# Loops exchanged so that products with 64 output rows alternate between the two halves of the array

## The chip, the cores and the metric

The kernel runs on one core of one Trainium2 chip. The number that counts is the device time of one execution in microseconds (us). Five engines work side by side and meet at semaphores: TensorE (PE, matrix products into PSUM, with its weight loads listed apart as PEld), VectorE (DVE), ScalarE (ACT), GpSimd (POOL) and SyncE (SP, which issues most transfers). TensorE is granted a clock at one of two levels, 2.4 GHz (shown as 1.00) or 1.2 GHz (0.50).

## What is computed

A two-layer encoder over 512 tokens of width 1024, in float32 at the interface. Layer 0 mixes by a convolution and a state-space model (SSM), layer 1 by attention in a neighbourhood; both end in a gated feed-forward network. Cut to the parts that matter here:

```python
# layer 0: depthwise convolution of width 31, and a scan in two directions
a = za * sigmoid(zg)
a = conv_general_dilated(a, conv_w, feature_group_count=512) + conv_b   # then layer norm, silu
s = associative_scan(affine, (A, B @ u))                                # 32 groups, 64 states
y = einsum(s_re, c_re) - einsum(s_im, c_im)                             # forward + backward, + d * u
# layer 1: 16 heads of 64, a query sees 8 grid rows x 16 grid columns
s = einsum('bhqd,bhjkd->bhqjk', q_r, k_blk) * scale + bias              # masked outside the window
p = softmax(s)
out = einsum('bhqjk,bhjkd->bhqd', p, v_blk)
# both layers
x = x + h;  x = x + (silu(h2 @ w_gate) * (h2 @ w_up)) @ w_down
```

## The kernel before

The program is one function, `tile_hybrid_encoder`, with helpers inside it. Its schedule is written by hand: instructions go to each engine's queue in the order of the Python code, and every engine works its queue in that order. A `Background` object only interleaves some VectorE work (the tables `Q` of the SSM output) with the loops, by a running credit. Large products are made in float32 pairs of a rounded part and a rest, three products each (`mm3`); the small products that the change touches are plain float32. In the trace each plain float32 product shows as two records of PE and two of PEld.

Three places make products with 64 output rows. In each, one PSUM tile of 128 partitions holds two independent results: output rows 0 to 63 come from the left half of the array's columns, rows 64 to 127 from the right half.

- **Convolution** (lines 991 to 1009). For each of 16 pairs of channel groups `n`, and for each half `h`, five products over the shifts `l` add up in `ps[64 * h:64 * h + 64, ...]`. The tables `t` (tiles `tca`, `tcb`) are made by ACT (line 763) or, for `TCV = 10`, by DVE (line 775), some groups ahead. After four groups DVE adds the bias (line 1006, tile `an` in the trace) and sums for the layer norm (line 1008).
- **SSM output**, `out_y` (lines 1014 to 1032). For each of four groups `gi` and each half, three products add up: one with the matrix `T` (line 1026) and two with `Q` (line 1028). It is called four times, with the layer norm's steps `ln_mean` and `ln_scale` between the calls; ACT copies the result (line 1031, `yn`).
- **Attention values**, `values` (lines 1372 to 1385). A unit `u` is a head pair `hp` (8 of them) and a quarter `j` of the queries (4), 32 units in all. For each head `e` of the pair, which is one half of the array, two blocks `b` of keys add up. The table `BLK` gives the blocks: for `j` = 1 and 2 both blocks have 128 keys, that is 128 rows of the array; for `j` = 0 the first block and for `j` = 3 the second has 64 keys, 64 rows of the array.

Attention is a pipeline over steps `s` (lines 1470 to 1484). In each step TensorE gets the transposes of unit `s-4` (`transp`, tile `t`, line 1364), the scores of unit `s` (tile `s`, line 1334) and the values of unit `s-6` (tile `o`, line 1379). DVE adds the bias and takes the row extreme (line 1341), ACT makes the exponentials (line 1344), DVE the reciprocal (line 1352) and POOL the scaling (line 1354). The transposed weights are copied to `pt_` (tile `sq`, two buffers) by ACT for `j` = 1, 2 (line 1366) and by DVE for `j` = 0, 3 (line 1369). The copy of unit `u` reuses the buffer of unit `u-2`, so it waits for that unit's values. After a head pair's fourth unit, DVE moves `o` to `qh` and `ql` (lines 1384, 1385). In the last six steps parts of the output projection (tile `wo`, lines 200 to 202) fill in between.

Of the kernel before, what the change touches and what calls it, by code (L numbers as in the profile page):

```python
# [30 lines left out]
P = 128  # L31
# [84 lines left out]
def tile_hybrid_encoder(ctx, tc, x, mix_norm, ffn_norm, ffn_w_gate, ffn_w_up, ffn_w_down,  # L116
# [5 lines left out]
    V, A, PE, PL = nc.vector, nc.scalar, nc.tensor, nc.gpsimd  # L122
# [51 lines left out]
    def psa(name="psa"):  # L174
        return psp.tile([P, 512], F32, tag="a", name=name, bufs=4)

    def psb(name="psb"):
        return psp.tile([P, 512], F32, tag="b", name=name, bufs=4)
# [3 lines left out]
    def xtile(name, dt=F32):  # L182

        i = xslot[0] % 10
        xslot[0] += 1
        if i < 8:
            return xp.tile([P, 512], dt, tag=f"x{i}", name=name)
        if i == 8:
            xpair_[:] = [xp.tile([P, 2, 512], dt, tag="x8", name=name)]
        return xpair_[0][:, i - 8]  # L190
# [83 lines left out]
    class Background:  # L274
# [20 lines left out]
        def tick(self, ns):  # L295
            self.credit = min(self.credit, CAP) + ns * self.share
            while self.credit > 0 and (self.jobs or self.fill):
                if self.jobs:
                    self.step()
                else:  # L300
                    self.step_fill()
# [31 lines left out]
    def pt(shape, name, pool=None, dt=F32):  # L333
        return (pool or mp).tile(shape, dt, tag=name, name=name)
# [274 lines left out]
    ps = psb("vec0")  # L609
# [12 lines left out]
    for k in range(KD):  # L622
        t = xtile("xT")
# [36 lines left out]
    for i in range(4):  # L660
# [7 lines left out]
        for kk in range(2):  # L668
            k = 2 * i + kk
            for j in range(4):  # L670
                c = slice(j * P, (j + 1) * P)
# [5 lines left out]
        if i == 1:  # L677
            make_pb(1)
            make_pb(2)
            ps = psb("vec")  # L680
# [10 lines left out]
            for t in range(LCH):  # L691
                p0 = 64 * (t % 2) + 16 * (t // 2)
# [4 lines left out]
        if i == 2:  # L697
            for r in range(2):
                ps = psb("ct")
# [66 lines left out]
    def make_tc(n):  # L766
        if n != TCV:
            for _ in g_tc(n):
                pass
            return  # L770
        t = slots[n // 2 % 3]
        for i in range(2):
            tcs[n + i] = t[:, :, i]
            for h in range(2):
                V.tensor_tensor(out=t[:, h, i], in0=wvs[:, h, n + i].unsqueeze(1).to_broadcast([P, 16, NLAG]),
                                in1=mask16.unsqueeze(2).to_broadcast([P, 16, NLAG]), op=ALU.mult)
# [10 lines left out]
    U = pt([P, G, NCH], "U")  # L787
# [17 lines left out]
    S2 = pt([P, 2, G, NCH], "S2")  # L805
# [126 lines left out]
    f, b = slice(0, 64), slice(64, 128)  # L932
# [18 lines left out]
    T = xp.tile([P, LCH, G, 16], F32, tag="xgl", name="T")  # L951
# [10 lines left out]
    Q = {i: lp.tile([P, 2, 8, 8, 16], F32, tag="Q", name="Q", bufs=4) for i in (0, 2, 1, 3)}  # L962
# [28 lines left out]
    for b in range(4):  # L991
        ps = psa("conv")
        for gi in range(4):
            n = 4 * b + gi
            t = tcs.pop(n)
            for h in range(2):
                for l in range(5):
                    PE.matmul(out=ps[64 * h:64 * h + 64, gi * P:gi * P + P],
                              lhsT=AC[:, 16 * h + n, l:l + NCH],
                              rhs=t[:, h, :, 8 * l:8 * l + 8],  # L1000
                              start=(l == 0), stop=(l == 4))
            if n % 2 and n + 5 < 16:
                make_tc(n + 5)
            tick(2200)
        gs = slice(4 * b, 4 * b + 4)
        V.tensor_tensor(out=yc[:, :, gs], in0=ps.rearrange("p (g c t) -> p t g c", g=4, t=LCH),
                        in1=cbB[:, gs].unsqueeze(1).to_broadcast([P, LCH, 4, 16]), op=ALU.add)
        V.tensor_reduce(out=lns[:, b], in_=yc[:, :, gs].rearrange("p t g c -> p t (g c)"), axis=AX.X, op=ALU.add)
        bgV.charge(1200)
# [4 lines left out]
    def out_y(i, hq, between=None):  # L1014
        for key in ((i, hq), (i + 2, hq)):
            if key in job_q:
                bgV.finish(job_q[key])
        ps = psb("y")
        for gi in range(4):
            if gi == 2 and between is not None:  # L1020
                between()
            for h in range(2):
                g = h * 16 + i * 8 + hq * 4 + gi
                o = ps[64 * h:64 * h + 64, gi * P:(gi + 1) * P]
                q8 = Q[g // 8]
                PE.matmul(out=o, lhsT=U[:, g], rhs=T[:, :, g], start=True, stop=False)
                for r in range(2):
                    PE.matmul(out=o, lhsT=S2[:, r, g],
                              rhs=q8[:, r, g % 8].rearrange("p t c -> p (t c)"),
                              start=False, stop=(r == 1))  # L1030
        A.activation(out=yn[:, :, i * 8 + hq * 4:i * 8 + hq * 4 + 4],
                     in_=ps.rearrange("p (g t c) -> p t g c", g=4, t=LCH), func=AF.Copy)
# [66 lines left out]
    def out_a(ct):  # L1099
# [9 lines left out]
        V.tensor_tensor(out=mal[:, ct], in0=y, in1=mah[:, ct].bitcast(F32), op=ALU.subtract)  # L1109

    out_y(0, 0)
    ln_mean()
    out_y(0, 1)
    for j in job_q.values():
        bgV.finish(j)
    W.ahead()
    out_y(1, 0, ln_scale)
    out_y(1, 1)
    ygs = mp.tile([P, 2, 4, S], F32R, tag="S2", name="ygs")
# [27 lines left out]
    for p2 in range(2):  # L1147
        wh, wl = W.next()
        W.ahead()
        for mi in range(2):  # L1150
            m = 2 * p2 + mi
            ps = psb("glu")
            for k in (0, 2, 1, 3):
                c = slice(mi * P, mi * P + P)
# [60 lines left out]
    for m in range(KD):  # L1215
        ps = psa("dn")
# [5 lines left out]
        t = xtile("x2")  # L1222
# [40 lines left out]
    def ring(name, dt=F32):  # L1263
        return ap_.tile([P, S], dt, tag="ring", name=name, bufs=6)
# [24 lines left out]
    def qk_post(qs, ssh, cg, psx):  # L1289

        isq = cg < 2
        for hp in range(4):
# [16 lines left out]
    BLK = {0: ((0, 64, 0, 0), (64, 128, 1, 0)), 1: ((0, 128, 1, 0), (128, 128, 2, 0)),  # L1309
           2: ((0, 128, 2, 0), (128, 128, 3, 0)), 3: ((0, 128, 3, 0), (128, 64, 0, 64))}  # L1310
# [61 lines left out]
    def values(u):  # L1372
        hp, j = units[u]
        pt_ = pts.pop(u)
        o = obank[hp % 2]
        for e in range(2):
            for b, (c0, n, kt, p0) in enumerate(BLK[j]):
                hc = (2 * hp + e) * 64
                PE.matmul(out=o[64 * e:64 * e + 64, j * P:(j + 1) * P], lhsT=vt[p0:p0 + n, kt, hc:hc + 64],  # L1379
                          rhs=pt_[p0:p0 + n, b, e], start=(b == 0), stop=(b == 1))  # L1380
        if j == 3:
            ov = o.rearrange("p (a r l) -> p a l r", l=16, r=8)[:, :, ::-1]
            hv, lv = (m_[:, hp].rearrange("p (a l r) -> p a l r", l=16, r=8) for m_ in (qh, ql))
            V.tensor_copy(out=hv, in_=ov)
            V.tensor_tensor(out=lv, in0=ov, in1=hv.bitcast(F32), op=ALU.subtract)

    for n, cg in enumerate(QKV_ORDER):
# [5 lines left out]
        for i in range(4):  # L1393
# [13 lines left out]
            for kk in range(2):  # L1407
                k = 2 * i + kk
                for j in range(4):
# [4 lines left out]
                    else:  # L1414
                        a, b = VSP[j - 1]
# [18 lines left out]
        else:  # L1434
            ssh = tmp([P, 4, 8], "ssh")
            qs = []
            for j in range(4):
                t = ring("qs")
# [31 lines left out]
    for s in range(2, NU + LV):  # L1470
        if 0 <= s - LT < NU:
            transp(s - LT)
        if s < NU:
            scores(s)
        if 0 <= s - LN < NU:
            normalize(s - LN)
        if 0 <= s - LV < NU:
            values(s - LV)
        if s == NU:
            out_proj(0, 0, 2)  # L1480
        if s == NU + 1:
            out_proj(0, 2, 4)
        if s == NU + 2:
            out_proj(0, 4, 7)
# [12 lines left out]
    for h in range(2):  # L1497
        for j in range(4):
            ps = psb("xn3")
# [3 lines left out]
            t = fp.tile([P, 512], F32, tag="xn3", name="xn3", bufs=4)  # L1503
# [3 lines left out]
        for i in range(NF // 2):  # L1507
# [5 lines left out]
            for kk, j in steps:  # L1513
                k = 2 * i + kk
                c = slice(j * P, (j + 1) * P)
# [4 lines left out]
        for j in range(4):  # L1520
            t = xn3[h, j]
# [30 lines left out]
```

## Time and profile before

| | us |
|---|---|
| median of 3 runs | 1246.53 (1246.44 to 1246.9) |
| the profiled execution | 1244.67 |
| its span, first to last instruction | 1242.9 |
| PE busy / PEld busy | 1212.7 / 961.6 |
| DVE busy / ACT busy / POOL busy | 671.6 / 473.8 / 38.5 |
| share of PE in the chain that ended last | 94% |

The span is 1.8 us shorter than the profiled execution's own time. PE busy counts records that overlap once, and their ends are modelled, so a busy PE need not be a PE at its best. The convolution and the SSM output lie between 135 and 193 us of the span, attention's pipeline between 753 and 832 us; the rest is almost all large products.

### The profile page before, as it was taken

How to read it: one execution, taken by the hardware profiler on the slowest of the kernel's cores; microseconds unless marked ns; L12 is line 12 of the kernel's file. 1: busy time of each engine (PE TensorE's matmuls, PEld its weight loads, DVE VectorE, ACT ScalarE, POOL GpSimd, SP SyncE). 2: the span in 40 equal slices, each digit the busy share in tenths (PEclk: the TensorE clock that was granted, in tenths of full speed). 3: DMA queues.
4: the chain of work that ended last, by engine and by line, in shares of the span. 5: the costliest groups of instructions: out<-in, count | busy, mean ns of one | idle time of the engine just before them, and what ended most of it. 6: DMA issues, size and time to landing. Idle time of an engine off the chain costs nothing.

```text
span 1242.9 us, 16156 instructions
## 1 busy us (share of the span) xinstructions
PE 1212.7 (98%) x6427; PEld 961.6 (77%) x6427; DVE 671.6 (54%) x1160; ACT 473.8 (38%) x835; POOL 38.5 (3%) x90
## 2 busy tenths in 40 slices
PE   7999869999999999999999999999999999999998
PEld 4655668888888888888888887678888888888886
DVE  8999787654444444333336654746544444452322
ACT  4556747532333232222234545634332332322120
POOL 1001000000000000000000002420000000000000
PEclk9999989999999999999999999999999999999999
DMA  7411402233333333333345442203233333323331
GB/s 159 92 52 57 118 1 80 91 102 102 94 93 95 92 102 98 93 94 94 102 136 169 136 131 91 86 18 102 85 102 102 102 90 97 90 96 102 119 102 34
DMA packets 173154, 118.04 MB, mean 95 GB/s; under 512 B 21193, under 2 KB 153593, under 8 KB 173080
## 3 DMA queue, kind: packets, MB, share of 16 engines
q1 hardware_dynamic: 172616, 115.92, 32.1%
q10 hardware_dynamic: 400, 1.07, 0.4%
q8 instruction: 50, 0.82, 0.3%
q14 instruction: 24, 0.20, 0.0%
q0 software_dynamic: 64, 0.03, 0.0%
HBM read 109.04 MB, written 7.96 MB: 94 GB/s over the span
## 4 chain that ended last, share of the span: by engine, by line
PE 94%; DVE 3%; ACT 2%; DMA 1%; issue 0%; SPq 0%; POOL 0%; POOLq 0%; DVEq 0%; ACTq 0%
PE up L200 6%; PE gate L201 6%; PE up L201 6%; PE gate L202 6%; PE up L202 6%; PE gate L200 6%; PE qkv L1417 4%; PE qkv L1418 4%; PE qkv L1419 4%; PE dn L202 3%; PE dn L201 3%; PE dn L200 3%; PE dn L1518 3%; PE dn L1516 3%; PE dn L1517 3%; PE o L1379 3%
## 5 line engine op out<-in xcount | busy, mean ns | idle before, releaser
L92 DVE TENSOR_TENSOR wlo<-wraw,whi 128x1024 fp32r<-128x1024 f32 x176 | 213.0, 1213 | 261.2 <-ACT whi L90 259.8
L90 ACT ACTIVATE whi<-wraw 128x1024 fp32r<-128x1024 f32 x176 | 183.4, 1044 | 283.1 <-issue 113.9
L200 PE MATMUL gate<-xgh,whi 128*128 128x512 f32 x352 | 137.2, 390 | 0.0
L200 PE MATMUL up<-xgh,whi 128*128 128x512 f32 x352 | 137.1, 390 | 0.0
L202 PE MATMUL gate<-xgh,wlo 128*128 128x512 f32 x352 | 137.0, 389 | 0.0
L202 PE MATMUL up<-xgh,wlo 128*128 128x512 f32 x352 | 137.0, 389 | 0.0
L201 PE MATMUL gate<-xgl,whi 128*128 128x512 f32 x352 | 136.9, 389 | 0.0
L201 PE MATMUL up<-xgl,whi 128*128 128x512 f32 x352 | 136.9, 389 | 0.0
L1201 DVE TENSOR_TENSOR fu<-up,rstdB 128x512 f32<-128x512 f32 x44 | 30.4, 691 | 113.3 <-PE up L202 113.3
L1203 ACT ACTIVATE gh<-fu 128x512 fp32r<-128x512 f32 x44 | 27.8, 632 | 150.8 <-DVE fu L1202 150.8
L200 PEld LDWEIGHTS gate<-xgh,whi 128*128 128x128 f32 x352 | 66.1, 188 | 13.9
L202 PEld LDWEIGHTS up<-xgh,wlo 128*128 128x128 f32 x352 | 66.1, 188 | 13.7
L201 PEld LDWEIGHTS gate<-xgl,whi 128*128 128x128 f32 x352 | 66.1, 188 | 13.7
L200 PEld LDWEIGHTS up<-xgh,whi 128*128 128x128 f32 x352 | 66.0, 188 | 13.7
L201 PEld LDWEIGHTS up<-xgl,whi 128*128 128x128 f32 x352 | 66.0, 188 | 13.7
L202 PEld LDWEIGHTS gate<-xgh,wlo 128*128 128x128 f32 x352 | 66.0, 188 | 13.6
L200 PE MATMUL dn<-gh,whi 128*128 128x512 f32 x176 | 69.3, 394 | 0.0
L201 PE MATMUL dn<-gl,whi 128*128 128x512 f32 x176 | 69.3, 394 | 0.0
L202 PE MATMUL dn<-gh,wlo 128*128 128x512 f32 x176 | 69.3, 394 | 0.0
L1518 PE MATMUL dn<-whi,gl 128*128 128x512 f32 x176 | 69.2, 393 | 0.0
L1516 PE MATMUL dn<-whi,gh 128*128 128x512 f32 x176 | 69.0, 392 | 0.0
L1417 PE MATMUL qkv<-whi,xgh 128*128 128x512 f32 x176 | 68.8, 391 | 0.0
(296 smaller groups left out, 2057.8 us busy)
## 6 DMA issues: line engine op xcount, KB each, us to landing
wraw<-in_ffn_w_gate_dram SPq DMA_DIRECT2D x44, 512.0 KB
wraw<-in_ffn_w_up_dram SPq DMA_DIRECT2D x44, 512.0 KB
wraw<-in_ffn_w_down_dram SPq DMA_DIRECT2D x38, 512.0 KB
wraw<-in_na_w_qkv_dram SPq DMA_DIRECT2D x24, 512.0 KB
wraw<-in_ab_w_in_dram SPq DMA_DIRECT2D x12, 512.0 KB
bt<-bd SPq DMA_DIRECT2D x8, 640.0 KB
wraw<-in_ab_w_out_dram SPq DMA_DIRECT2D x8, 512.0 KB
wraw<-in_na_w_out_dram SPq DMA_DIRECT2D x8, 512.0 KB
```

What stands on the lines that cost most here:

```text
L90: self.nc.scalar.activation(out=hi, in_=raw, func=AF.Copy)
L92: eng.tensor_tensor(out=lo, in0=raw, in1=hi.bitcast(F32), op=ALU.subtract)
L200: PE.matmul(out=o, lhsT=lh, rhs=rh, start=start, stop=False)
L201: PE.matmul(out=o, lhsT=lh, rhs=rl, start=False, stop=False)
L202: PE.matmul(out=o, lhsT=ll, rhs=rh, start=False, stop=stop)
L1379: PE.matmul(out=o[64 * e:64 * e + 64, j * P:(j + 1) * P], lhsT=vt[p0:p0 + n, kt, hc:hc + 64], rhs=pt_[p0:p0 + n, b, e], start=(b == 0), st ...
L1417: PE.matmul(out=pq[j], lhsT=lh, rhs=wh[:, kk], start=(k == 0), stop=False)
L1418: PE.matmul(out=pq[j], lhsT=lh, rhs=wl[:, kk], start=False, stop=False)
L1419: PE.matmul(out=pq[j], lhsT=ll, rhs=wh[:, kk], start=False, stop=(k == 7))
L1516: PE.matmul(out=pd[j], lhsT=gh[:, k, c], rhs=wh[:, kk], start=(k == 0), stop=False)
L1517: PE.matmul(out=pd[j], lhsT=gh[:, k, c], rhs=wl[:, kk], start=False, stop=False)
L1518: PE.matmul(out=pd[j], lhsT=gl[:, k, c], rhs=wh[:, kk], start=False, stop=(k == NF - 1))
```

## The change

In all three places the loop over the halves becomes the inner one. The same products are made with the same operands, and each half's sum is built in the same order; only the order in which the two halves' products stand in TensorE's queue is new. The queues of DVE, ACT, POOL and SP are the same, instruction by instruction.

```diff
-            for h in range(2):
-                for l in range(5):
+            for l in range(5):
+                for h in range(2):
                     PE.matmul(out=ps[64 * h:64 * h + 64, gi * P:gi * P + P],
...
-            for h in range(2):
-                g = h * 16 + i * 8 + hq * 4 + gi
-                o = ps[64 * h:64 * h + 64, gi * P:(gi + 1) * P]
-                q8 = Q[g // 8]
-                PE.matmul(out=o, lhsT=U[:, g], rhs=T[:, :, g], start=True, stop=False)
-                for r in range(2):
-                    PE.matmul(out=o, lhsT=S2[:, r, g],
-                              rhs=q8[:, r, g % 8].rearrange("p t c -> p (t c)"),
+            gs = [h * 16 + i * 8 + hq * 4 + gi for h in range(2)]
+            o = [ps[64 * h:64 * h + 64, gi * P:(gi + 1) * P] for h in range(2)]
+            for h, g in enumerate(gs):
+                PE.matmul(out=o[h], lhsT=U[:, g], rhs=T[:, :, g], start=True, stop=False)
+            for r in range(2):
+                for h, g in enumerate(gs):
+                    PE.matmul(out=o[h], lhsT=S2[:, r, g],
+                              rhs=Q[g // 8][:, r, g % 8].rearrange("p t c -> p (t c)"),
                               start=False, stop=(r == 1))
...
-        for e in range(2):
-            for b, (c0, n, kt, p0) in enumerate(BLK[j]):
+        for b, (c0, n, kt, p0) in enumerate(BLK[j]):
+            for e in range(2):
                 hc = (2 * hp + e) * 64
                 PE.matmul(out=o[64 * e:64 * e + 64, j * P:(j + 1) * P], lhsT=vt[p0:p0 + n, kt, hc:hc + 64],
```

TensorE's queue at the end of attention, before and then in the change (`t` transposes, `o` values, `wo` output projection; the two last units' values are units 30 and 31). This is the one unit whose waits let the order be seen, since the products of all other units read alike:

```order
@@ -2914,6 +2879,8 @@
 L1379 MATMUL o<-sq,vt 64x128 [waits Activation_49]
 L1379 MATMUL o<-sq,vt 64x128 x3
-L1379 MATMUL o<-sq,vt 64x128 [waits DVE_49] x2
-L1379 MATMUL o<-sq,vt 64x128 x2
+L1379 MATMUL o<-sq,vt 64x128 [waits DVE_49]
+L1379 MATMUL o<-sq,vt 64x128
+L1379 MATMUL o<-sq,vt 64x128 [waits DVE_49]
+L1379 MATMUL o<-sq,vt 64x128
 L200 MATMUL wo<-qh,whi 128x512
 L201 MATMUL wo<-ql,whi 128x512
```

The wait for the second block's copy moved from the second product of unit 31 to the third: both halves of the first block now stand ahead of both halves of the second. The same exchange is made in each of the 32 units.

TensorE's queue at the first call of `out_y`, before (the two buffers of `Q` are those of the two halves):

```order
L1026 MATMUL y_1716<-T_1376,U_523 64x128
L1028 MATMUL y_1716<-Q_1384,S2_524 64x128 x2
L1026 MATMUL y_1716<-T_1376,U_523 64x128
L1028 MATMUL y_1716<-Q_1385,S2_524 64x128 x2
L1026 MATMUL y_1716<-T_1376,U_523 64x128
```

and in the change, where line 1025 is the product with `T`:

```order
L1025 MATMUL y_1716<-T_1376,U_523 64x128 x2
L1028 MATMUL y_1716<-Q_1384,S2_524 64x128
L1028 MATMUL y_1716<-Q_1385,S2_524 64x128
L1028 MATMUL y_1716<-Q_1384,S2_524 64x128
L1028 MATMUL y_1716<-Q_1385,S2_524 64x128
```

Three products of one half and three of the other became six that alternate.

## Rows read from the trace of the kernel before

**Rows 1.** The page: busy time of each engine; shares of the chain by engine.

```profile
PE 1212.7 (98%) x6427; PEld 961.6 (77%) x6427; DVE 671.6 (54%) x1160; ACT 473.8 (38%) x835; POOL 38.5 (3%) x90
...
PE 94%; DVE 3%; ACT 2%; DMA 1%; issue 0%; SPq 0%; POOL 0%; POOLq 0%; DVEq 0%; ACTq 0%
```

**Rows 2.** Windows, one head pair: PE, PEld, DVE, ACT, POOL busy (count), PEclk, DMA share.

```profile
777.20:785.70 8.50, 8.50 (x78) 5.65 (x73) 5.92 (x27) 5.12 (x18) 3.54 (x8) 1.00 0.25 77
```

**Rows 3.** Chain of waits, same head pair: start us, us, what.

```profile
776.85 0.59 PE o L1379 x8
...
778.58 1.44 PE o L1379 x8
...
781.16 1.44 PE o L1379 x8
...
783.70 0.59 PE o L1379 x8
```

**Rows 4.** Timeline of PEld: start, us, line, operation, tiles, array rows*columns.

```profile
781.09 0.19 PEld L1379 LDWEIGHTS o<-sq,vt 64*64 64x64 f32 x2
781.45 0.19 PEld L1379 LDWEIGHTS o<-sq,vt 128*64 128x64 f32 x2 [0.17 <-issue]
...
782.53 0.42 PEld L1364 LDWEIGHTS t<-ident,e 128*128 128x128 f32 x4 [0.17 <-issue]
...
783.63 0.42 PEld L1379 LDWEIGHTS o<-sq,vt 128*64 128x64 f32 x8
```

**Rows 5.** Timeline of PE from 783.62 to 783.70 us, columns as in rows 4.

```profile
783.63 0.34 PE L1379 MATMUL o<-sq,vt 128*64 128x128 f32 x2
```

**Rows 6.** Line 1379: its products by shape; one of those who waited (us, times).

```profile
L1379 PE MATMUL o<-sq,vt x256: 269/273/324, 764.1 to 831.7; 128*64 128x128 f32 x96, 64*64 64x128 f32 x32
...
  DVE sq L1369: 20.1, 8
```

**Rows 7.** Chain of waits at the end of attention.

```profile
830.34 0.43 PE o L1379 x2
...
830.80 1.15 PE o L1379 x6
831.95 0.43 PE wo L200
```

**Rows 8.** Line 998, the convolution: idle of PE before it; who waited (nobody).

```profile
  ACT tca L763: 7.5, 7
  ACT tcb L763: 7.0, 2
who waited for it (us, times):
```

**Rows 9.** Chain of waits around the SSM output.

```profile
181.10 0.59 PE mean L1067 x2
...
187.53 0.60 ACT yn L1031
188.13 0.95 ACT whi L90
...
195.36 1.79 PE cT L1093 x29
```

**Rows 10.** Timeline of PE at the start of the second `out_y`.

```profile
181.63 0.69 PE L1026 MATMUL y<-T,U 128*64 128x128 f32 x2
...
182.11 0.48 PE L1026 MATMUL y<-T,U 128*64 128x128 f32 x1
```

**Rows 11.** Windows around the SSM output, columns as in rows 2.

```profile
180.00:185.00 5.00, 3.90 (x32) 3.87 (x34) 3.37 (x4) 2.01 (x10) 0.00 (x0) 0.50 0.01 3
...
190.00:195.00 5.00, 3.59 (x64) 3.35 (x60) 4.59 (x19) 1.22 (x4) 0.00 (x0) 1.00 0.61 193
195.00:200.00 5.00, 4.64 (x71) 4.33 (x71) 3.22 (x7) 4.92 (x10) 0.00 (x0) 1.00 0.07 22
```

**Rows 12.** Timeline of PE: products with 64 output rows that already alternate between halves.

```profile
122.42 1.15 PE L882 MATMUL v<-U,un_ppb 128*64 128x64 f32 x32
```

## The prediction

> **What bounds the kernel now.** I read the page first. PE is busy for 98% of the span and holds 94% of the chain that ended last [rows 1], so a gain has to be TensorE time at a place where TensorE is what everyone waits for. Busy time alone doesn't tell whether products run side by side, so I went to the three places that the change touches, and at each asked two questions: do the two halves of the array overlap already, and does anyone wait for the result?
>
> Attention. In the windows view TensorE is busy for all 8.50 us that a head pair (four units) takes; DVE has 5.92 us of work in that time, ACT 5.12, POOL 3.54 [rows 2]. The windows of the head pairs before and after it read alike. DVE's copies waited 20.1 us for the values [rows 6]. So TensorE sets the pace. The chain shows what it does with the time: the eight records of one unit's values (four float32 products, two records each) take either 0.59 us or 1.44 us, in the rhythm 0.59, 1.44, 1.44, 0.59 [rows 3]. The weight loads tell the two kinds apart. In a long unit there are four groups of two loads, 0.36 us from one to the next, and the shape changes from 64 to 128 array rows at every group: 781.09, 781.45, and so on to the transposes at 782.53 [rows 4]. These are `j` = 0 and 3, where one block has 64 keys. In a short unit (`j` = 1, 2) all eight loads have 128 rows and go through in one run of 0.42 us [rows 4]. There the two halves do run side by side, although the old order gives all of one half before the other: the first two records, one of each half, together span 0.34 us from their start, hardly longer than the 0.32 that one record lasts at most [rows 5, 6]. So TensorE overlaps halves across several products already. It pays at each change of the number of rows, where nothing of the next shape starts until the last is through.
>
> Convolution. TensorE sat idle for 7.5 and 7.0 us ahead of it until ACT had its tables, and nobody waited for its result [rows 8].
>
> SSM output. After the layer norm's mean product at 181.10 the chain goes through the second call of `out_y`, at the lower clock of 1.2 GHz (granted 0.50 [rows 11]), to ACT's copy `yn` at 187.53, and on through the weight split to the transposes at 195.36 [rows 9]. Here it is on the path.
>
> **The change part by part.** No instruction is added or removed, and only TensorE's queue has another order, so no other queue is passed.
>
> Values, `j` = 1 and 2 (16 units). Eight records already overlap in 0.59 us; both orders have one shape and no change of rows. I take 0 and bound it at 0.1 us a unit either way, 1.6 us in all.
>
> Values, `j` = 0 and 3 (16 units; 32 of the 128 products have 64 rows, two in each of them [rows 6]). The old order has the shapes 64, 128, 64, 128, and at 0.36 us a group that is 4 x 0.36 = 1.44 us. The new order has two groups, each with both halves. If the second half rides along, as in the short units, a group costs its 0.36 plus the lag between halves, 0.02 at most (0.34 less 0.32 [rows 5, 6]); I take 0.37, so the unit costs 0.74 and saves 0.70 us. Bounds: the new unit can't be shorter than a short one, 0.59, which saves 0.85; and each group holds half of a short unit's records, so if it cost as much as a whole short unit, the unit would take 1.18 and save 0.26. I stay with 0.70, since a group of 0.36 is measured with the very shapes, and the overlap with one of them. Over 16 units: 11.2 us, between 4.2 and 13.6.
>
> The Trainium skill, in "TensorE: Matmul & The Clock Gate", part 3 ("What overlaps and what doesn't"), says that a weight load overlaps a running product only where the row groups differ. By that rule two halves that share their rows could not overlap, the new unit would still need its 1.44 us, and the sum would lose the 11.2. The run of eight loads in 0.42 us [rows 4] is against it; the rule is a rival below.
>
> Is the time then TensorE's to give? A head pair shrinks from 8.50 to 8.50 - 2 x 0.70 = 7.10 us. DVE's 5.92 us still fit, with 1.2 to spare, ACT and POOL more easily. DVE waits for the values before its copies for `j` = 0, 3, and the bias steps stand behind these copies in its queue; but TensorE overwrites a unit's scores only two steps later, 2 x 7.10 / 4 = 3.6 us, and the seven records of two copies, two bias steps and a reciprocal are about 1.5 us by DVE's mean of 5.92 / 27 = 0.22 a record [rows 2]. The bias loads use 0.25 of the transfer engines over 8.50 us [rows 2], 2.1 us of 7.10. So I let no other engine take back anything; if DVE's waits bring a head pair to 7.6, eight of them return 4 us. The last unit stands behind DVE's copies: its eight records ran from 830.34 to 831.95, and the second block's copy released the rest at 830.80 [rows 7]. In the new order the first block is through by 830.71 and the second ends at 830.80 + 0.37 = 831.17, again 0.7 earlier.
>
> SSM output. The old order lets the first half run alone until the second half's first product starts 0.48 us later (182.11 against 181.63 [rows 10]). The new one starts both at once, and the call's 48 records end that much sooner: 0.5 us on the chain, bounds 0 and 0.5. The other calls end ahead of ACT's turn. The layer norm's mean, which starts this stretch, waits for DVE and not for TensorE.
>
> Convolution. Alternating shortens its PE time, and all of that falls into PE's idle time [rows 8]: 0. Its cover is ACT's table making; without that cover the convolution would give a few us more, but ACT's order is the same.
>
> Clock. More idle time ahead of the SSM output can change when the clock falls or rises. If the rest of the SSM output and what follows it up to 200 us ran at the lower level, their PE time of 3.59 + 4.64 us [rows 11] could double, of which 5.00 - 3.59 = 1.4 us fall into a wait; at most 6.8 us are lost. If the second `out_y` got the full clock instead, about half of its 5.9 us (181.63 to 187.53 [rows 9, 10]), 2.9 us, would be won. I take 0.
>
> Sum: 11.2 + 0.5 = 11.7 us. Of the profiled execution's 1244.67 us this leaves 1232.97. The median of the runs is 1.86 us above that execution, and the forecast is for the median: 1246.53 - 11.7 = 1234.8 us.
>
> **The rivals.**
> 1. The halves don't overlap at 64 rows. All rows on overlap in line 1379 are for 128 array rows; the 64-row groups never had the other half beside them. Then a 64-row group costs two single ones, 0.72, the unit 1.09, and 16 units save 5.6 us: 1246.53 - 6.1 = 1240.4. For it: that shape is untested. Against it: nothing in the 128-row rows points to a reason.
> 2. Another engine takes over. DVE would go from 70% to 83% of the time; with 4 us returned: 1238.8.
> 3. The lower clock reaches past 188.5 us. At half of the 6.8 us above this gives 1234.8 + 3.4 = 1238.2, at most 1241.6. For it: the SSM stage already has the lower level once, and PE will idle more ahead of it. Against it: before, the clock was back at 1.00 by 190 us [rows 11], while PE worked.
> 4. Nothing happens in attention: halves with equal rows overlap only when a run of one half ends, and the pairs stay one after the other. 1246.53 - 0.5 = 1246.0. The rule of the Trainium skill named above gives this too. Against it: 32 records that alternate went through in 1.15 us [rows 12].
> 5. Slower: each change of half makes TensorE drain, as each change of rows does. The place is `j` = 1 and 2, where the new order has three changes of half instead of one. At 0.36 us a group the unit goes from 0.59 to 1.44, 16 x 0.85 = 13.6 us, and the long units gain nothing: 1246.53 + 13.6 = 1260.1. It decides as soon as a change of half costs over 0.70 / 4 = 0.18 us, since there are two more of them in a short unit and two in a long one, against 0.70 us gained. [rows 12] speak strongly against it, with a product every 0.07 us in alternation.
>
> **How the numbers follow.** Forecast 0.76, rival 1 0.07, rival 2 0.06, rival 3 0.05, rival 4 0.03, rival 5 0.03. The forecast's own bounds are 1246.53 - 13.6 - 0.5 = 1232.4 and, with 0.6 us a unit and nothing from the SSM output, 1236.9; I widen the lower one to 1232 for the clock. The upper end goes to 1240, which takes in rivals 2 and 3 and stops at rival 1. A measurement of this kernel can tell about 0.2% (2.5 us) from no change. Forecast and rivals 1 to 3 are all faster by more than that, 0.94; rival 4 is within it, 0.03; rival 5 slower, 0.03.
>
> **What would show it.** In the changed profile the values of all units should take about 0.59 or 0.74 us in the chain and no longer 1.44, with two groups of four weight loads where there were four of two in the long units; a head pair should take about 7.1 us with PE still busy throughout; the convolution should be shorter and PE's idle time before it longer by as much; the second `out_y` should take about 5.4 us from its first product to `yn`, where it took 5.9. A head pair of over 7.4 us with gaps on PE would speak for rival 2, units of 1.09 for rival 1, a granted clock of 0.50 past 188.5 us for rival 3. The prediction is wrong if two halves with 64 array rows exclude each other, or if alternation itself costs.

## The result, and the profile after

The changed kernel takes 1233.01 us (median of four, 1232.66 to 1234.7) where the kernel before takes 1246.49 (median of four, three of them the runs of the table ahead of the prediction): ratio 0.9897, 95% interval 0.9885 to 0.9909. A second set gives 1233.59 against 1245.84, ratio 0.9902 (0.9887 to 0.9917). It is faster by 13.5 us in the first set and by 12.3 us in the second. The profiled execution took 1232.86 us, its span is 1231.1 us against 1242.9: 11.8 us shorter, where the sum had 11.7. One run of experiment e4 below took 1512.51 us at a mean granted clock of 0.75, and e4's ratio leaves it out.

First the page of the changed kernel: busy time of each engine, and the chain's shares. Compare [rows 1].

```profile
PE 1194.9 (97%) x6427; PEld 949.4 (77%) x6427; DVE 670.8 (54%) x1160; ACT 473.1 (38%) x835; POOL 37.5 (3%) x90
...
PE 94%; DVE 3%; ACT 2%; DMA 0%; issue 0%; SPq 0%; POOL 0%; POOLq 0%; DVEq 0%
```

PE's busy time fell by 17.8 us with the same 6427 records, which is more than the span lost: most of the other 6 us came out where PE waits anyway (the convolution, below). The chain is still TensorE's by 94%, so the freed time was not handed to another engine.

Next one head pair of attention in the windows view (columns as in [rows 2]):

```profile
773.40:780.50 7.10, 7.10 (x75) 4.91 (x73) 5.83 (x27) 5.02 (x18) 3.82 (x9) 1.00 0.30 92
```

The same work that took 8.50 us takes 7.10, and PE fills it without a gap. DVE is busy for 5.83 of the 7.10 and still follows. The chain of waits shows the four units of one head pair (start us, us, what; `o` are the values, compare [rows 3]):

```profile
767.15 0.59 PE o L1379 x8
...
768.88 0.73 PE o L1379 x8
...
770.76 0.74 PE o L1379 x8
...
772.60 0.59 PE o L1379 x8
```

The two units that took 1.44 us take 0.73 and 0.74; the short ones are at 0.59, as before. Why, is in the timeline of the weight loads (PEld; start us, us, line, operation, tiles, array rows*columns):

```profile
768.81 0.20 PEld L1379 LDWEIGHTS o<-sq,vt 128*64 128x64 f32 x4
769.18 0.20 PEld L1379 LDWEIGHTS o<-sq,vt 64*64 64x64 f32 x4 [0.17 <-issue]
769.55 0.42 PEld L1364 LDWEIGHTS t<-ident,e 128*128 128x128 f32 x4 [0.17 <-issue]
...
770.69 0.20 PEld L1379 LDWEIGHTS o<-sq,vt 64*64 64x64 f32 x4
771.06 0.20 PEld L1379 LDWEIGHTS o<-sq,vt 128*64 128x64 f32 x4 [0.17 <-issue]
...
772.53 0.42 PEld L1379 LDWEIGHTS o<-sq,vt 128*64 128x64 f32 x8
```

Where [rows 4] had four groups of two loads, there are two groups of four. From one group to the next it is 0.37 us (768.81, 769.18, 769.55), whether a group holds two loads or four: the second half rides along. The 64-row group behaves like the 128-row one.

Those who waited for the values wait less. DVE's copies, 20.1 us in [rows 6], in the view of line 1379 now:

```profile
  DVE sq L1369: 11.1, 8
```

At the end of attention the chain reads (compare [rows 7]):

```profile
819.28 0.44 PE o L1379 x4
819.74 0.43 PE o L1379 x4
820.17 0.43 PE wo L200
```

What is left once the second block's copy is there takes 0.43 us where it took 1.15.

The SSM output in the chain (compare [rows 9]), and the first products of the second `out_y` in PE's timeline (compare [rows 10]):

```profile
181.15 0.60 PE mean L1067 x2
181.75 0.63 PE y L1025 x4
...
187.12 0.60 ACT yn L1031
...
194.93 1.80 PE cT L1093 x29
```

```profile
181.68 0.70 PE L1025 MATMUL y<-T,U 128*64 128x128 f32 x4
```

Both halves start with the first group (four records from 181.68 on, where there were two until 182.11). From the first product to `yn` it is 5.44 us, where it was 5.90, and `cT` starts 0.43 us earlier.

The convolution, as one group of four channel pairs in PE's timeline, before and then after:

```profile
139.07 3.44 PE L998 MATMUL conv<-tca,AC 128*64 128x128 f32 x40 [0.48 <-ACT tca L763]
```

```profile
139.11 2.40 PE L998 MATMUL conv<-tca,AC 128*64 128x128 f32 x40 [0.85 <-ACT tca L763]
```

Forty records take 2.40 us instead of 3.44, the one place where alternation itself does much. What it brings to the time is read from the windows of the whole convolution, before and then after (PE is the first number behind the comma):

```profile
135.00:171.00 36.00, 29.32 (x354) 28.02 (x354) 32.16 (x49) 31.11 (x92) 0.84 (x1) 0.95 0.30 67
```

```profile
135.00:171.00 36.00, 24.73 (x369) 23.03 (x368) 32.16 (x49) 31.15 (x92) 0.84 (x1) 0.91 0.31 65
```

PE's 4.6 us less of work became 4.6 us more of idling, and ACT's 31.1 us did not move. The granted clock fell from 0.95 to 0.91: there is one more stretch at the lower level, from 157.0 to 160.4 us. It is hidden like the rest. What hides it is VectorE's queue as well as ACT's tables: from 156.5 us to the mean product the chain of waits is DVE's work alone, the last convolution table, the tables `Q`, the bias and the sums. These are the ends of that stretch in the changed kernel; before, it ran from 156.43 to the mean at 181.10 [rows 9].

```profile
156.47 3.02 DVE tcb L775 x4
...
180.41 0.70 DVE lns L1008
```

Where the 11.8 us of the span went, by the start times of the products that end each stage (the last record of the layer norm's `mean`, the first `cT`, the first `gate`, the last product of `qkv`, the last of `o`); some of the experiments below stand beside them:

| | mean to `cT` | `cT` to gate | last `qkv` to last `o` | span |
|---|---|---|---|---|
| before | 14.02 | 57.83 | 72.76 | 1242.9 |
| after | 13.54 | 57.79 | 61.44 | 1231.1 |
| after, second set | 12.96 | 59.06 | 61.43 | 1231.6 |
| e1 | 13.03 | 60.57 | 61.43 | 1233.2 |
| e2 | 12.65 | 60.52 | 72.74 | 1244.0 |
| e3 | 14.01 | 59.13 | 72.74 | 1244.1 |
| e4 | 13.72 | 59.12 | 67.18 | 1238.1 |
| e5 | 13.83 | 59.10 | 59.13 | 1230.1 |
| e6, e6 again | 12.80, 12.66 | 60.62, 59.04 | 59.23, 59.23 | 1230.8, 1229.7 |
| e7 | 12.45 | 60.55 | 61.44 | 1232.8 |
| e8 | 12.46 | 60.63 | 61.46 | 1233.3 |
| e9 | 12.46 | 60.17 | 59.23 | 1229.6 |
| e10 | 13.11 | 57.91 | 59.23 | 1228.5 |

Attention gave 11.32 us and the stretch behind the mean 0.48; every other stage is equal to 0.05 us. The third column moves only when the values' code moves, by hundredths otherwise. The first two also move from one execution to the next by up to 2.8 us, with the granted clock, and that has to be kept apart from what an edit does.

### The profile page after: what moved, and what is told of

It is laid out like the page before. It is cut to its first block, busy times and chain, and to the rows that moved or that the text cites. A ratio compares the mean times of both kernels' runs of the same rounds, so it can differ in the third digit from the quotient of the medians.

```text
span 1231.1 us, 16156 instructions
## 1 busy us (share of the span) xinstructions
PE 1194.9 (97%) x6427; PEld 949.4 (77%) x6427; DVE 670.8 (54%) x1160; ACT 473.1 (38%) x835; POOL 37.5 (3%) x90
## 4 chain that ended last, share of the span: by engine, by line
PE 94%; DVE 3%; ACT 2%; DMA 0%; issue 0%; SPq 0%; POOL 0%; POOLq 0%; DVEq 0%
PE up L200 7%; PE gate L202 6%; PE up L202 6%; PE gate L200 6%; PE gate L201 6%; PE up L201 6%; PE qkv L1417 4%; PE qkv L1419 4%; PE qkv L1418 4%; PE dn L201 3%; PE dn L202 3%; PE dn L200 3%; PE dn L1518 3%; PE dn L1516 3%; PE dn L1517 3%; PE wo L200 2%
```

## The experiments

**Which of the three places.** e1, e2 and e3 each make one of the three exchanges in the kernel before.

> The kernel before with the exchange in the attention values alone. Theory (fewer changes of row count, with the two halves overlapping): attention's pipeline 11.3 us shorter, all of it on the path, so a ratio of about 0.991 and a span of about 1231.6 us. Rival (part of the gain comes from the convolution or the SSM output): clearly less, a span of 1233 us or more.

```diff
-        for e in range(2):
-            for b, (c0, n, kt, p0) in enumerate(BLK[j]):
+        for b, (c0, n, kt, p0) in enumerate(BLK[j]):
+            for e in range(2):
```

Measured: 1234.08 us, ratio 0.9907 (0.989 to 0.9923). Attention is 11.33 us shorter, all of what the whole change gave there. The span is 2.1 us longer than after's, and by the sign that I had set, a span of 1233 us or more, the rival had come. The stages deny it, since none of the 2.1 us is in attention: the stretch between `cT` and gate took 60.57 us. The windows on either side of 195 us say why (columns as in [rows 2]; the granted clock is the last number but two), first of after, then of e1:

```profile
181.00:195.00 14.00, 12.07 (x149) 11.64 (x150) 8.13 (x22) 7.42 (x23) 0.00 (x0) 0.76 0.23 75
195.00:205.00 10.00, 10.00 (x94) 8.56 (x95) 6.96 (x12) 9.53 (x18) 0.00 (x0) 1.00 0.02 5
```

```profile
181.00:195.00 14.00, 12.13 (x160) 11.70 (x161) 8.03 (x21) 8.07 (x25) 0.00 (x0) 0.85 0.24 77
195.00:205.00 10.00, 10.00 (x77) 8.63 (x75) 7.60 (x13) 9.53 (x16) 0.00 (x0) 0.66 0.01 2
```

In e1 the clock came back earlier (185.2 instead of 187.7 us) and fell once more, from 195.5 to 202.3: PE was busy for all 10 us and got 77 records through instead of 94 (some of the difference is that e1's `cT` began 0.7 us earlier; in the 10 us from the first `cT` on, 81 records start instead of 94). e1 doesn't touch anything ahead of attention, so this is not the edit's doing. The kernel before scatters in the same way: over the seven executions of it beside e7 and e8, the mean granted clock goes from 0.994 down to 0.990 while the span goes from 1242.8 up to 1244.8 us. The mean over the whole span is a weak sign, though: beside e1 there are executions of 1243.2 us at 0.994 and of 1244.7 us at 0.993, and beside e10 one of 1243.2 us at 0.991. What counts is where the low stretch lies, in a wait or in work.

> The kernel before with the exchange in the SSM output alone. Theory: the stretch from the layer norm's last mean product to the first transposes of the mixer (lines 1067 to 1093) is 0.4 to 0.5 us shorter and nothing else moves, a span of about 1242.4 us. Rival (the gain there is the clock's, not the order's): no shortening unless the granted clock of that stretch differs.

```diff
-            for h in range(2):
-                g = h * 16 + i * 8 + hq * 4 + gi
...
+            for r in range(2):
+                for h, g in enumerate(gs):
...
```

Measured: 1245.76 us in a single run, span 1244.0. Mean to `cT` is 12.65 us, 1.37 shorter than before, but the clock came back at 184.1 us, where before it came back at 187.6: granted 0.78 against 0.53 in the same 7 us (e2, then before).

```profile
181.00:188.00 7.00, 7.00 (x92) 6.78 (x94) 2.75 (x3) 5.17 (x19) 0.00 (x0) 0.78 0.01 2
```

```profile
181.00:188.00 7.00, 6.90 (x64) 6.87 (x65) 2.40 (x3) 3.77 (x17) 0.00 (x0) 0.53 0.01 2
```

So this run can't tell the order of the products from the clock, and it is inconclusive on the 0.48 us.

> The kernel before with the exchange in the convolution alone. Theory: the convolution's products take some 6 us less of TensorE's busy time, TensorE waits for ScalarE's tables longer by as much, and the mean product comes at the same time to 0.1 us: span 1242.9 us. Rival (TensorE holds the tables' buffers and so delays ScalarE): the tables and the layer norm come earlier. The added idle time may also move where the granted clock falls.

```diff
-            for h in range(2):
-                for l in range(5):
+            for l in range(5):
+                for h in range(2):
```

Measured: 1245.83 us in a single run, span 1244.1. In the convolution's window PE is busy as little as in the whole change (4.4 us less than before in this window, where I had expected some 6 in all), and the layer norm's mean starts 0.1 us from where it did before.

```profile
135.00:171.00 36.00, 24.97 (x368) 23.34 (x366) 32.17 (x49) 31.02 (x92) 0.84 (x1) 0.91 0.31 64
```

The convolution's gain is hidden behind ACT's tables and DVE's queue, and ACT gets nothing out of it. The 1.2 us by which this span is longer lie between `cT` and gate, at a lower clock from 197.5 to 200.9 us.

**Is it the alternation, or the number of row changes?** In the change both come together. e4 keeps alternation but has three groups of rows in a long unit instead of two: for `j` = 0, 64 rows, then 128 for both halves, then 64 again, and for `j` = 3 the same with 64 and 128 exchanged.

> The kernel before, but in the units with a 64-key block the four products go left half 64 rows, right half 128 rows, left half 128 rows, right half 64 rows: the half changes nearly every time, the number of rows twice instead of three times. Theory (a change of the number of rows is what costs, about 0.36 us a group): three groups, 1.09 us a unit, 0.35 us less than before, 16 units, 5.6 us: a span of about 1237.3 us. Rival (alternating halves is what helps by itself): 0.74 us a unit, as in the changed kernel, a span of about 1231.6 us.

```diff
-        for e in range(2):
-            for b, (c0, n, kt, p0) in enumerate(BLK[j]):
+        order = ((0, 0), (1, 1), (0, 1), (1, 0)) if j in (0, 3) else ((0, 0), (0, 1), (1, 0), (1, 1))
+        seen = [0, 0]
+        for e, b in order:
+            c0, n, kt, p0 = BLK[j][b]
...
```

Measured: 1239.87 and 1240.44 us, ratio 0.9956 (0.9937 to 0.9975). e4's chain and weight loads:

```profile
778.32 1.09 PE o L1381 x8
...
780.55 1.09 PE o L1381 x8
```

```profile
780.48 0.19 PEld L1381 LDWEIGHTS o<-sq,vt 64*64 64x64 f32 x2
780.84 0.20 PEld L1381 LDWEIGHTS o<-sq,vt 128*64 128x64 f32 x4 [0.17 <-issue]
781.21 0.19 PEld L1381 LDWEIGHTS o<-sq,vt 64*64 64x64 f32 x2 [0.17 <-issue]
```

Three groups, 0.36 and 0.37 us apart, make a unit of 1.09 us: 1.44, 1.09 and 0.74 for four, three and two groups. Attention gave 5.58 us, half of the change's 11.32. The halves alternate throughout, so alternation is not what pays here; each group less does.

e5 goes the other way: the old order, one half after the other, but every block read with 128 rows.

> The kernel before in its old order (one half's two products, then the other's), but the 64-key blocks are multiplied with 128 rows, the second operand being that of the other block, so that the attention's values are other numbers while the number of products stays. Theory (the change of the number of rows is what costs): all 32 units take 0.59 us without any alternation, 16 x 0.85 = 13.6 us less, a span of about 1229.3 us, if VectorE follows a head pair of 6.8 us. Rival (the old order itself keeps the halves apart): the units stay at 1.44 us, a span of 1242.9 us. A third (VectorE takes over below 7.1 us): units short, but with idle time on TensorE, a span of 1230.5 us or more.

```diff
-            for b, (c0, n, kt, p0) in enumerate(BLK[j]):
+            for b in range(2):
+                kt = BLK[j][b][2]
+                src = b if BLK[j][b][1] == 128 else 1 - b
...
-                PE.matmul(out=o[64 * e:64 * e + 64, j * P:(j + 1) * P], lhsT=vt[p0:p0 + n, kt, hc:hc + 64],
-                          rhs=pt_[p0:p0 + n, b, e], start=(b == 0), stop=(b == 1))
+                PE.matmul(out=o[64 * e:64 * e + 64, j * P:(j + 1) * P], lhsT=vt[:, kt, hc:hc + 64],
+                          rhs=pt_[:, src, e], start=(b == 0), stop=(b == 1))
```

Measured: 1231.4 us, ratio 0.9885 (0.9865 to 0.9905); attention 13.63 us shorter, though the 32 products of 64 rows got twice the rows. e5's chain, and its window of one head pair:

```profile
776.82 0.59 PE o L1381 x8
...
778.55 0.59 PE o L1381 x8
```

```profile
775.00:781.80 6.80, 6.80 (x74) 4.99 (x72) 5.80 (x27) 5.06 (x18) 3.52 (x8) 1.00 0.31 96
```

Every unit of this head pair is a short one without any alternation. The window also answers rival 2 beyond what the change asked: at 6.80 us a head pair, with DVE busy for 5.80, PE still has no gap.

**A version that uses this.** e6 is the changed kernel with the 64-key blocks padded to 128 rows, by a copy of the values in which the other 64 rows are zero.

> The changed kernel, and the 64-key blocks padded to 128 rows: the values' edge tile is kept twice, with zeros in the other half of its rows, and the weights of the neighbouring keys fall on the zeros. Two more copies of 64 rows on ScalarE and small fills on GpSimd. Theory: units of 0.59 instead of 0.74 us, 16 x 0.15 = 2.4 us less than the changed kernel, a span of about 1228.8 us. Rival (the other engines take back what is left): no less than the changed kernel's 1231.1 us.

> The changed kernel once more, as the measure for the padded one on the same chip. Theory: a ratio of 0.990 to 0.991 to the kernel before, spans of about 1231 us; where its time varies from run to run, it is the granted clock of the SSM stage that differs. Rival (the 13.5 us between the medians are the gain): a ratio of 0.989.

> The padded kernel once more, as the measure for the one with the products that fill the waits. Theory: attention's stretch as before to 0.05 us, a ratio of about 0.988 to 0.989; its time moves from run to run with the granted clock between 175 and 205 us. Rival (something else moves it): stretches other than the one from the mean product to the first gate product differ between the two profiles of this kernel.

```diff
-    BLK = {0: ((0, 64, 0, 0), (64, 128, 1, 0)), 1: ((0, 128, 1, 0), (128, 128, 2, 0)),
-           2: ((0, 128, 2, 0), (128, 128, 3, 0)), 3: ((0, 128, 3, 0), (128, 64, 0, 64))}
+    BLK = {0: ((0, 128, 0, 0), (64, 128, 1, 0)), 1: ((0, 128, 1, 0), (128, 128, 2, 0)),
+           2: ((0, 128, 2, 0), (128, 128, 3, 0)), 3: ((0, 128, 3, 0), (64, 128, 4, 0))}
...
+                if j == 0:
+                    A.activation(out=vt[0:64, 0, vc], in_=pq[0][0:64], func=AF.Copy, scale=rst[0:64, 4:5])
+                    A.activation(out=vz[cg - 4][64:128], in_=pq[0][64:128], func=AF.Copy, scale=rst[64:128, 4:5])
+                    continue
```

Measured: 1231.94 us, ratio 0.9886 (0.9869 to 0.9902); in a second set 1231.32 and 0.9883 (0.9867 to 0.99). The change again, beside e6's first set on the same chip, gave the 1233.59 named above. The long units of e6 are short now (its chain):

```profile
777.51 0.59 PE o L1383 x8
...
779.24 0.59 PE o L1383 x8
```

Attention is another 2.2 us shorter than in the change (59.23 against 61.43), 16 times the 0.14 us between a long unit and a short one. The stage's times show it in both executions; the whole times' intervals overlap, since the clock between 180 and 205 us scatters by as much. For the same reason the spans of e4, e5 and e6 came out 0.8 to 2.0 us above the ones expected: the excess lies between `cT` and gate.

**Can that clock be had?** Ahead of the layer norm's last mean product PE waits for DVE: between 173 and 181 us it is busy for 0.6 of 8.0 us, before and after. e7 fills this with nine products that nobody reads.

> The changed kernel, and nine products of 512 columns whose result nobody reads ahead of the layer norm's mean product (line 1067), where TensorE waits for VectorE from about 171 to 181 us. Theory (what differs from run to run is the granted clock of the mixer stage): the clock stays at 1.00 up to the second output call, the stretch from the mean product to the first gate product is 2 to 4 us shorter than the 71.3 us of the changed kernel, and the times of the runs lie closer together. Rival (the clock is not what that stretch waits for): the stretch keeps its length.

```diff
+        fill = psb("fill")
+        for _ in range(9):
+            PE.matmul(out=fill, lhsT=ident, rhs=U[:, 0:8].rearrange("p g k -> p (g k)"), start=True, stop=True)
```

Measured: 1234.21 us, ratio 0.9906 (0.989 to 0.9923), no better than the change. e7's windows:

```profile
171.00:181.00 10.00, 9.08 (x36) 4.51 (x32) 9.69 (x16) 0.60 (x1) 0.00 (x0) 1.00 0.00 0
181.00:195.00 14.00, 10.02 (x164) 9.50 (x166) 8.31 (x22) 8.22 (x25) 0.00 (x0) 0.99 0.24 78
195.00:205.00 10.00, 10.00 (x75) 8.68 (x73) 7.67 (x13) 9.50 (x16) 0.00 (x0) 0.68 0.00 1
```

The clock is full over the SSM output, and mean to `cT` falls by 1.09 us. But PE's work there is done sooner, it waits for DVE and ACT (10.02 busy of 14.00 us, in after 12.07), and the clock falls at 194.6 until 201.4 us, in the stretch where PE has no slack: `cT` to gate costs 2.76 us more. The expected gain of 2 to 4 us is not there. Its runs do lie closer together, as expected: 1.1 us from lowest to highest, against 2.0 in each set of the change. The chain shows a second thing:

```profile
181.33 0.40 PE mean L1070 x2
...
183.01 1.15 ACT diag L1078 x5
184.23 2.09 ACT diag L1078 x10
186.32 0.48 ACT yn L1031
```

At the full clock `out_y` isn't on the path any more; ACT's `diag` is. e8 asks what the order of `out_y` is worth there: e7 with the old order of that one function.

> As the kernel with the nine products, but with the SSM output in its old order. Theory: at the full clock the half that runs ahead costs half of what it cost at the lower one, so the stretch from the mean product to the first transposes is 0.2 to 0.25 us longer than with the new order. Rival (the order of the SSM output gives nothing, the clock all): equal to 0.05 us.

```diff
-            for r in range(2):
-                for h, g in enumerate(gs):
...
+            for h in range(2):
+                g = h * 16 + i * 8 + hq * 4 + gi
...
```

Measured: 1234.35 us, ratio 0.9909 (0.9894 to 0.9924); mean to `cT` 12.46 against 12.45. My 0.2 to 0.25 us was wrong, for the reason in e7's chain; e8's goes through `diag` too. The 0.48 us of the change are there because the clock is low.

e9 is e6 with e7's fill, e10 is e9 with three more such products behind the last `out_y`, in PE's next wait.

> The kernel with the padded blocks, and the nine products. Theory: both gains add, 2.2 us from attention and 2 to 4 us from the clock, a ratio of about 0.985 to 0.987 to the kernel before. Rival (the clock falls elsewhere instead): no better than the padded kernel's 0.9886.

> As the kernel with the padded blocks and the nine products, and three more products that nobody reads between the last SSM output and the first transposes of the mixer (line 1093), where TensorE waited for VectorE for 3.1 us and the granted clock fell right after. Theory (the clock falls where TensorE has little to do, and what it costs is the work that stands behind): the clock stays at 1.00 through the transposes, the stretch from them to the first gate product goes from 60.2 us back to 57.8 us or less, and the stretch from the mean product keeps its 12.46 us: a span of about 1227.2 us. Rival (the transposes themselves bring the clock down): the clock falls again before 200 us and the span stays at 1229.6 us or more.

```diff
+    fill = psb("fill")
+    for _ in range(3):
+        PE.matmul(out=fill, lhsT=ident, rhs=U[:, 0:8].rearrange("p g k -> p (g k)"), start=True, stop=True)
```

e9 measured 1232.24 us, ratio 0.989 (0.9876 to 0.9905), with the clock down from 192.7 to 199.5. The 0.985 to 0.987 that I expected were not there; the rival came. e10 measured 1229.88 us, ratio 0.9873 (0.9859 to 0.9888), beside e6 again on the same chip with 0.9883. e10's windows:

```profile
181.00:195.00 14.00, 13.87 (x164) 11.77 (x165) 8.10 (x22) 7.94 (x24) 0.00 (x0) 0.88 0.26 78
195.00:205.00 10.00, 10.00 (x90) 8.45 (x89) 7.47 (x13) 9.41 (x16) 0.00 (x0) 1.00 0.00 1
```

From 195 us on the clock is full and `cT` to gate is at 57.91, as expected. But the clock was low from 182.6 to 186.0, with the first fill in place, and mean to `cT` took 13.11 us where I had expected 12.46. Its chain shows what held `cT` there:

```profile
191.67 2.77 PE fill L1124 x6
194.44 1.75 PE cT L1096 x29
```

The low clock made the `out_y` calls end later, and the three products behind them then filled more than PE's wait: PE had no gap left, and the transposes stood behind the fill instead of behind DVE. Up to the last `out_y` e9 and e10 give TensorE the same queue, so the stretch at 182.6 is not the three products' doing, and one profile can't tell whether they kept the clock full behind 195 us. e10 has the lowest median of all and beats the kernel before by 15.6 us, but its interval overlaps those of the change and of e6. Beside e6 again, its four runs (1229.19 to 1230.19) all lie below e6's four (1230.26 to 1231.44). That speaks for a gain of some 1.4 us from the fills, but with four runs each, and e9 no better than e6, it is not settled.

## Why the prediction was right, point by point

- **Attention, the long units.** Right in mechanism and size: 0.73 to 0.74 us where I had 0.74, 11.32 us where I had 11.2. Rival 1 (units of 1.09, and 64 rows without overlap) is denied by the four 64-row loads in one 0.20 us run. e4 and e5 show the reason that the prediction only argued: the price is per group of equal rows, whatever the order of the halves.
- **The short units.** 0.59 in either order, as taken. Rival 5, alternation that drains, is denied by them, and by the convolution's 2.40 us.
- **The rule on overlap.** The eight loads of a short unit share their rows between two halves and go through in 0.42 us, and the four of a long unit's group in 0.20. The Trainium skill ("TensorE: Matmul & The Clock Gate", part 3, "What overlaps and what doesn't") lets a load overlap a running product only where the row groups differ. The traces do not agree for halves of the columns, and rival 4, which followed from it, is denied by the units' 0.73 us.
- **The price of a row change.** A group costs 0.36 to 0.37 us with two records or four, in the kernel before, after and in e4. The Trainium skill ("TensorEngine Tiling (Array Packing)", "Key Properties") says that a change of the tiling mode drains TensorE; the 0.17 us without a weight load that the rows show at the changes of shape within a unit agree with that. Whether TensorE is empty by then, as I wrote, the rows can't show, because the ends of products are modelled.
- **Other engines.** Nothing was taken back: PE is busy for 7.10 of 7.10 us, and rival 2 would not even have come with e5's 6.80.
- **The end of attention.** 0.7 us predicted, 0.72 measured (1.15 to 0.43); the two times in the prediction, 831.95 and 831.17, are 0.78 apart.
- **SSM output.** 0.48 us in the profiled execution where I had 0.5. The size holds only as long as the clock is low over the whole `out_y`: with the full clock it is 0 (e7, e8). Between the two lie e1 (old order) and e6 (new order), where the clock came back at almost the same place, 185.2 and 185.3 us, 4.0 us behind the mean: 13.03 against 12.80 us, so 0.23 us for the order. The lower bound, 0, is where the term goes when its condition is gone; I had not named that condition.
- **Convolution.** 0 is right, but the cover that I named is only the first of two. ACT's tables hold the stretch up to 156.5 us; from there to the mean it is DVE's queue, which I had left out. So my "without that cover the convolution would give a few us more" is not shown. A detail of my reading was off, too: I called the 7.5 and 7.0 us of [rows 8] idle time of PE, but the window of 135 to 171 us has only 36.00 - 29.32 = 6.7 us without PE at work. So the source view's sum can't be taken as PE's idle time; most likely it counts a wait for the weight load and for the product: of its 7.0 us behind `tcb`, in two waits, PE's timeline has one of 3.39 us.
- **The clock.** Rival 3 had the right place and the wrong cause. In the changed kernel's profiled execution the clock came back at 187.7 us, as before at 187.6, though PE idles more. In other executions it comes back earlier and falls again behind 194 us, for 1.3 to 2.8 us more between `cT` and gate; but e1, which leaves everything ahead of attention alone, does that as well. The upside of 2.9 us was too large: with the old order, e8's full clock brings mean to `cT` from 14.02 to 12.46 us, 1.6 us, since ACT's `diag` then takes over the path.
- **The median.** Forecast 1234.8, measured 1233.0. The step that was off is the one that set the sum against the median: I assumed that the median stands as far above the profiled execution as it did before (1.86 us). After the change it stands 0.15 us above, in the second set 0.20. The trace accounts for 11.8 us; the medians differ by 13.5 and, in the second set (1245.84 to 1233.59), by 12.3. The rest is of the size of the clock's scatter, and part of it is the base: 1246.53 was the median of three runs, while the four later sets of the kernel before have medians of 1245.52 to 1245.84. The second set's interval, 0.9887 to 0.9917, still leaves room for a gain of 13.5 us. The measured time lies only 1 us above the lower end of my range. That end allowed for long units of 0.59 us, which did not come, so the scatter fell into room that was made for something else. Whether the change also makes the better course of the clock more frequent is open; I did not test it.

## What to carry to other kernels

Where small products of different row counts follow each other on a TensorE that never idles, count the groups of equal shape rather than the products: here each group less was worth 0.36 us, and filling a 64-row block up to 128 rows was cheaper than changing shape. Before counting on an overlap, look at how many weight loads go through in one run. And before an end-to-end difference of 1 or 2 us is given to an edit, compare the stage that was edited and the granted clock of those that were not.

## What I had not expected of the hardware

- Halves overlap although they are queued apart, but only so far. Two products of one half and then two of the other (values) take 0.59 us in either order. Five and five (convolution) take 3.44 us for 40 records in the old order and 2.40 alternating, at the full clock.
- I had said that every engine works its queue in order. TensorE does not start products of the two halves so. In the old `out_y` the first half's product with `T` (line 1026) and its two with `Q` (line 1028), six records in all, stand ahead of the second half's product with `T`. Behind the first half's two records of line 1026 (181.63 in [rows 10]), PE's timeline of the kernel before goes on:

```profile
182.11 0.42 PE L1028 MATMUL y<-Q,S 128*64 128x128 f32 x1
182.11 0.48 PE L1026 MATMUL y<-T,U 128*64 128x128 f32 x1
182.32 0.42 PE L1028 MATMUL y<-Q,S 128*64 128x128 f32 x1
```

The record of line 1026 at 182.11 is the second half's first. It starts beside the first of four records of the first half's `Q` and ahead of the other three.
- Giving the 32 products of 64 rows twice the rows made attention shorter (e5, e6), since nothing then breaks a unit's run of one shape.
- Keeping PE busy ahead of the SSM output did not remove the low clock. The low stretch came later, from 194.6 us (e7) and 192.7 us (e9), or was shorter, 182.6 to 186.0 us (e10).
